# Which four PSUM sums stay in place across the value phases of a product-key retrieval kernel, and which bank the rotation takes first

## Chip, core and metric

The kernel runs on 1 core of one Trainium2 chip. The metric is the device time of one execution in microseconds (us). TensorE is PE in the rows (PEld for its weight loads), VectorE is DVE, ScalarE is ACT, GpSimd is POOL, SyncE is SP. PSUM has eight banks; a bank holds 512 float32 per partition.

## What is computed

One decoder layer with a gated recurrence, a short convolution and, after them, a retrieval from 16384 single-neuron experts. The change lies in the retrieval:

```python
def block(xb):                                  # 128 tokens at a time
    ...                                         # top 16 experts of each of 8 heads: idx, and their softmax gate
    u = expert_u[idx]
    v = expert_v[idx]
    act = gelu(einsum('td,thkd->thk', xb, u))
    return einsum('thk,thkd->td', gate * act, v)
```

1024 tokens, width 1024, all in float32; products are made of halves (a rounded high part and the rest), so each product of two matrices is three matmuls.

## The kernel before

The first 672 tokens are handled densely: for each of 128 blocks of 128 experts the kernel multiplies all 672 tokens with the block's `u` rows, applies Gelu, multiplies with a mostly empty matrix of gates, and multiplies the result W with the block's `v` rows. The other 352 tokens are handled by gathering each token's own rows (`L1084` on POOL, two kinds of row products on DVE in `L1094` and `L1102`); this work runs beside the dense work, in five row buffers.

The dense stage, about 1264 to 2964 us of the profile, alternates two things on PE.

- **U blocks** (`u_steps`, `L1163`): for one block of experts two groups of 24 matmuls, one over 384 tokens and one over 288 (the two parts of `SPL`), each in a bank of the pool `pa`, which has two banks. ACT reads each with Gelu (`L1168`) into the tile `Wl`. Forty of the blocks (`EARLIES`) were done earlier and are loaded from DRAM (`ged`). Then DVE multiplies with the gates (`L1384`), ACT makes the high half `Wh` (`L115`) and DVE the low half `Wl` (`L116`).
- **Value phases** (`v_phase`, `L1403`): for three blocks of experts, 16 groups, one for each token part j and each 128 columns c of the width, of 9 matmuls each (three blocks, three products of halves). The order is j = 0, c = 0 to 7 (384 tokens), then j = 1, c = 0 to 7 (288 tokens). Here they are called groups 0 to 15.

A phase comes between two U blocks, one block behind, so that two (late in the stage three) U blocks lie between phases. Four of the 16 groups are in `FIXED`: each has a bank of its own (`pacc`) and goes on summing through all phases, and DVE has nothing to do for it until the end. The other twelve take a bank in turn from `new_pv`, alternately one of the two `pa` banks and one of the two `pv` banks, and DVE adds each to its sum in SBUF (`L1419`); until that is done, the bank is not free. So a `pa` bank is used by U blocks and phases in turn, and a `pv` bank by phases alone.

Each engine works off its own queue in order. The order in those queues comes from a scheduler in the compiler's tile layer, which places instructions by its own estimate of when they can start. The gathering work is handed out along the dense matmuls (`along`, `advance`).

Of the kernel before, what the change touches and what calls it, by code (L numbers as in the profile page):

```python
# [61 lines left out]
WB = 2  # L62
WJ = 0
PAIRS = [(0, 2), (2, 4)]
FIXED = [(0, 1), (0, 5), (1, 1), (1, 5)]
RB = 0.15
RD = 0.0
DG = 2
# [31 lines left out]
def build(tc, A, out, dbg=None):  # L100
# [41 lines left out]
    with root:  # L142
# [1200 lines left out]
        while u_early(1.0, "G"):  # L1343
# [7 lines left out]
        accs = {(j, c): mp.tile([P, n], F32, name=f"acc{j}{c}") for j, (_, n) in enumerate(SPL) for c in range(KC)  # L1351
                if (j, c) not in FIXED}
        fixed = {f: psM.tile([P, 512], F32, name=f"pacc{f[0]}{f[1]}", bufs=1) for f in FIXED}

        turn = [0]

        def new_pv():

# [182 lines left out]
```

## Time and profile before

| | |
|---|---|
| time, median of 3 runs (lowest to highest) | 2999.6 us (2998.78 to 3002.16) |
| the profiled execution's own time | 2986.61 us |
| its span, first to last instruction | 2984.8 us |
| busy in the span: PE, DVE, ACT, POOL | 95%, 85%, 31%, 29% |
| dense stage, 1264 to 2968 us: PE busy, DVE busy | 1629.70, 1526.58 of 1704.00 us |
| granted TensorE clock in that stage | 0.99 of full speed |

Busy time of PE counts matmuls as pipelined, so it is not work at its peak. A wait shown for an engine is idle time just before an instruction, with the instruction that ended it; waits of PEld and PE for the same thing lie over each other and are not added.

### The profile page before, as it was taken

To read this page: it belongs to the slowest core of one execution; us is meant where nothing else is said; L and a number is where in the kernel's file an instruction comes from. 1 tells how busy PE (TensorE), PEld (TensorE's weight loads), DVE (VectorE), ACT (ScalarE), POOL (GpSimd) and SP (SyncE) were. 2 spreads that over 40 slices of the span, in tenths; PEclk is the share of its full clock that TensorE was granted. 3 is DMA by queue.
4 is the path that set the end of the run, shared out by engine and by line. 5 is a ranking of instruction groups with operands and counts; after the bars stand their busy time and mean duration, and the time that the engine had idled before them with its cause. 6 is when DMAs were issued, how large, how long until landed. Compare 5 with 4: busy or idle time off the path is not lost.

```text
span 2984.8 us, 47174 instructions
## 1 busy us (share of the span) xinstructions
PE 2850.0 (95%) x18190; PEld 2687.0 (90%) x18190; DVE 2547.3 (85%) x5369; ACT 939.3 (31%) x1548; POOL 862.6 (29%) x726
## 2 busy tenths in 40 slices
PE   8999999989999999999999999999899999899998
PEld 6887898878999889999999999999899999899998
DVE  6885549988999987488999989889899988899998
ACT  5643645333222455422222222222222222222222
POOL 0000000000000000045554544445454554555451
PEclk9999999989999999999999999999999999999999
DMA  7424342244223687788889989899899998899995
GB/s 271 146 90 140 127 155 64 78 141 146 70 90 112 212 253 244 246 307 323 324 324 330 340 321 340 325 323 332 304 351 327 329 324 316 311 327 329 324 320 182
DMA packets 288676, 740.01 MB, mean 248 GB/s; under 512 B 27873, under 2 KB 122081, under 8 KB 282050
## 3 DMA queue, kind: packets, MB, share of 16 engines
q0 software_dynamic: 102944, 374.78, 35.3%
q1 hardware_dynamic: 185506, 362.22, 35.3%
q8 instruction: 142, 2.33, 0.3%
q14 instruction: 84, 0.69, 0.1%
HBM read 666.29 MB, written 70.52 MB: 247 GB/s over the span
## 4 chain that ended last, share of the span: by engine, by line
issue 27%; DVE 25%; DMA 20%; PE 20%; POOL 5%; ACT 2%; SPq 0%; DVEq 0%; POOLq 0%; ACTq 0%
PE pp L469 5%; DVE gacc L1094 5%; DMA wl<-in_uT 3%; DVE wl L116 3%; DVE acc L1419 3%; DMA Wl<-ged 2%; PE pq L875 2%; PE pp L875 2%; DVE vl L116 2%; DVE Wl L1384 1%; DMA more<-in_u,idx 1%; PE pa L1163 1%; PE ps L579 1%; PE pp L380 1%; POOL more L1084 1%
## 5 line engine op out<-in xcount | busy, mean ns | idle before, releaser
L1163 PE MATMUL pa<-h2h,wh 128*128 128x384 f32 (+1 forms) x1840 | 590.3, 321 | 14.2 <-DVE acc L1419 12.0
L1163 PE MATMUL pa<-h2l,wh 128*128 128x384 f32 (+1 forms) x1840 | 588.0, 320 | 0.0
L1163 PE MATMUL pa<-h2h,wl 128*128 128x384 f32 (+1 forms) x1840 | 584.0, 317 | 2.7 <-DVE wl L116 2.7
L1163 PEld LDWEIGHTS pa<-h2h,wh 128*128 128x128 f32 x1840 | 347.9, 189 | 19.4 <-DVE acc L1419 13.3
L1163 PEld LDWEIGHTS pa<-h2h,wl 128*128 128x128 f32 x1840 | 349.0, 190 | 2.9 <-DVE wl L116 2.9
L1163 PEld LDWEIGHTS pa<-h2l,wh 128*128 128x128 f32 x1840 | 349.7, 190 | 0.0
L115 ACT ACTIVATE Wh<-Wl 128x672 fp32r<-128x672 f32 x128 | 98.0, 766 | 754.4 <-PE pv L1403 487.9
L115 ACT ACTIVATE wh<-wl 128x1024 fp32r<-128x1024 f32 x187 | 197.7, 1057 | 385.6 <-DMA wl<-in_uT 187.1
L1403 PE MATMUL pa<-Wh,vh 128*128 128x384 f32 (+1 forms) x768 | 251.5, 327 | 53.6 <-ACT Wl L1168 41.7
L116 DVE TENSOR_TENSOR wl<-wl,wh 128x1024 fp32r<-128x1024 f32 x187 | 228.0, 1219 | 75.3 <-ACT wh L115 74.6
L1403 PE MATMUL pv<-Wh,vh 128*128 128x384 f32 (+1 forms) x768 | 245.4, 320 | 5.2 <-DVE acc L1419 4.9
L1403 PE MATMUL pa<-Wl,vh 128*128 128x384 f32 (+1 forms) x768 | 245.8, 320 | 0.7 <-DVE Wl L116 0.7
L1403 PE MATMUL pa<-Wh,vl 128*128 128x384 f32 (+1 forms) x768 | 245.6, 320 | 0.0
L1403 PE MATMUL pv<-Wh,vl 128*128 128x384 f32 (+1 forms) x768 | 243.7, 317 | 0.0
L1403 PE MATMUL pv<-Wl,vh 128*128 128x384 f32 (+1 forms) x768 | 243.3, 317 | 0.0
L1403 PEld LDWEIGHTS pa<-Wh,vh 128*128 128x128 f32 x768 | 145.7, 190 | 67.7 <-ACT Wl L1168 52.1
L115 ACT ACTIVATE vh<-vl 128x1024 fp32r<-128x1024 f32 x128 | 134.4, 1050 | 125.5 <-DMA vl<-in_v 75.5
L1403 PE MATMUL pacc<-Wh,vh 128*128 128x384 f32 (+1 forms) x512 | 163.6, 320 | 1.5 <-ACT vh L115 1.5
L1403 PE MATMUL pacc<-Wh,vl 128*128 128x384 f32 (+1 forms) x512 | 163.7, 320 | 0.6 <-DVE vl L116 0.6
L1403 PE MATMUL pacc<-Wl,vh 128*128 128x384 f32 (+1 forms) x512 | 163.0, 318 | 0.0
L116 DVE TENSOR_TENSOR vl<-vl,vh 128x1024 fp32r<-128x1024 f32 x128 | 155.7, 1217 | 3.2 <-ACT vh L115 3.2
L469 PE MATMUL pp<-h1h,wh 128*128 128x512 f32 x384 | 157.3, 410 | 0.0
(1944 smaller groups left out, 7405.8 us busy)
## 6 DMA issues: line engine op xcount, KB each, us to landing
wl<-in_uT SPq DMA_DIRECT2D x128, 512.0 KB, 5.9
vl<-in_v SPq DMA_DIRECT2D x128, 512.0 KB, 7.9
gd<-stg SPq DMA_DIRECT2D x21, 2048.0 KB, 9.3
gsb<-gd SPq DMA_DIRECT2D x32, 1344.0 KB, 9.1
wl<-in_win SPq DMA_DIRECT2D x48, 512.0 KB, 3.5
wa<-in_wada SPq DMA_DIRECT2D x16, 1024.0 KB, 5.0
wl<-in_wq SPq DMA_DIRECT2D x32, 512.0 KB, 3.5
ged<-ge SPq DMA_DIRECT2D x40, 336.0 KB, 3.1
```

Source lines behind the costliest of these rows:

```text
L115: C.activation(hi, src, AF.Copy)
L116: V.tensor_tensor(lo, src, hi.bitcast(F32), op=OP.subtract)
L380: T.matmul(pvs[t], l[:, t * P:(t + 1) * P], r, start=(k == 0 and l is h1[0][k] and r is wi[0]), stop=(k == KC - 1 and l is h1[1][k]))
L469: T.matmul(pp, l[:, k], r[k], start=(i == 0), stop=(i == 3 * KC - 1))
L579: T.matmul(ps_[:, c], X[:, cs_], Y[:, cs_], start=True, stop=True)
L875: T.matmul(pq[:, :m], l[:, k], hs[k, r][:, o:o + m], start=(i == 0), stop=(i == 3 * KC - 1))
L1084: G.indirect_dma_start(out=r, out_offset=None, in_=src, in_offset=IndirectOffsetOnAxis(ap=idx[:n, s0 + j:s0 + j + 1], axis=0))
L1094: V.scalar_tensor_tensor(ac, r, aw[:, j:j + 1], ac, op0=OP.mult, op1=OP.add))
L1163: T.matmul(pa[:, :n], l[:, k], h2[k, r][:, o:o + n], start=(i == 0), stop=(i == 3 * KC - 1))
L1384: V.tensor_tensor(gv, gv, gs[b // GB][:, :, b % GB], op=OP.mult)
L1403: T.matmul(pv[:, :n], l[:, c * P:(c + 1) * P], r[:, o:o + n], start=(i == 0 and (not fx or b0 == 0)), stop=(i == 3 * (b1 - b0) - 1 and (no ...
L1419: V.tensor_tensor(a, a, pv[:, :n], op=OP.add)
```

## The change

Two constants. The four fixed groups are (j, c) = (0, 0), (0, 1), (1, 6), (1, 7), so groups 0, 1, 14 and 15 of a phase, and no longer groups 1, 5, 9 and 13. And the turn starts at 1, so that a phase's first rotating group takes a `pv` bank and not a `pa` bank.

```diff
-FIXED = [(0, 1), (0, 5), (1, 1), (1, 5)]
+FIXED = [(0, 0), (0, 1), (1, 6), (1, 7)]
...
-        turn = [0]
+        turn = [1]
```

No instruction is added or removed; the order in the queues changes. Before, the rotating groups of a phase are 0, 2, 3, 4, 6, 7, 8, 10, 11, 12, 14, 15 and take pa, pv, pa, pv and so on; now they are groups 2 to 13 and take pv, pa, pv, pa and so on.

The first place is PE at the start of a phase: the last matmul of the U blocks, and the first of each of the first groups. Before:

```order
L1163 MATMUL pa<-h2h_86,wl 128x288
L1403 MATMUL pa<-Wh,vh 128x384
...
L1403 MATMUL pacc_13127<-Wh,vh 128x384
...
L1403 MATMUL pv<-Wh,vh 128x384
```

Now:

```order
L1163 MATMUL pa<-h2h_86,wl 128x288
L1403 MATMUL pacc_13127<-Wh,vh 128x384
...
L1403 MATMUL pacc_13128<-Wh,vh 128x384
...
L1403 MATMUL pv<-Wh,vh 128x384
...
L1403 MATMUL pa<-Wh,vh 128x384
```

The first `pa` bank of a phase was that of group 0 and is that of group 3.

The second place is DVE between the U blocks and the first add of a phase (the phase that begins at 1943.31 us in the profile of before). `Wl<-Wl,gsb` is the product with the gates, `Wl<-Wl,Wh` the low half of W, `wl` and `vl` low halves of `u` and `v`, `grow` and `more` are gathered rows. Before:

```order
L1384 TENSOR_TENSOR Wl<-Wl,gsb 128x672
L1102 SCALAR_TENSOR_TENSOR grow__19770,aw<-grow__19770,hx 128x1024
L116 TENSOR_TENSOR Wl<-Wl,Wh 128x672
L1102 SCALAR_TENSOR_TENSOR grow__19786,aw<-grow__19786,hx 128x1024
L1102 SCALAR_TENSOR_TENSOR grow__19802,aw<-grow__19802,hx 128x1024
L116 TENSOR_TENSOR vl<-vl,vh 128x1024
L116 TENSOR_TENSOR wl<-wl,wh 128x1024
L1384 TENSOR_TENSOR Wl<-Wl,gsb 128x672
L1419 TENSOR_TENSOR acc_13115<-acc_13115,pa 128x384
```

Now:

```order
L1384 TENSOR_TENSOR Wl<-Wl,gsb 128x672
L1102 SCALAR_TENSOR_TENSOR grow__19770,aw<-grow__19770,hx 128x1024
L1102 SCALAR_TENSOR_TENSOR grow__19786,aw<-grow__19786,hx 128x1024
L116 TENSOR_TENSOR Wl<-Wl,Wh 128x672
L1102 SCALAR_TENSOR_TENSOR grow__19802,aw<-grow__19802,hx 128x1024
L116 TENSOR_TENSOR vl<-vl,vh 128x1024
L1102 SCALAR_TENSOR_TENSOR more,aw<-more,hx 128x1024
L1384 TENSOR_TENSOR Wl<-Wl,gsb 128x672
L1102 SCALAR_TENSOR_TENSOR grow__19850,aw<-grow__19850,hx 128x1024
L116 TENSOR_TENSOR Wl<-Wl,Wh 128x672
L116 TENSOR_TENSOR wl<-wl,wh 128x1024
L1419 TENSOR_TENSOR acc_13115<-acc_13115,pv 128x384
```

The first add stands three instructions later, and the first `Wl<-Wl,Wh`, the half that the phase itself needs, stands one row product later.

## Rows read from the trace of the kernel before

**Rows 1.** The stage 1264 to 2968 us: length, then busy us per engine.
```profile
1264.00:2968.00 1704.00, 1629.70 (x10334) 1605.08 (x10335) 1526.58 (x2169) 390.80 (x559) 847.95 (x698) 0.99 0.89 320
```

**Rows 2.** Waits in the dense stage: engine, waiter, releaser: us, times, longest.
```profile
PEld pa L1403 <- ACT Wl L1168: 52.1, 41, 3.2
PE pa L1403 <- ACT Wl L1168: 41.7, 34, 3.0
PEld pa L1403 <- DVE acc L1419: 15.1, 14, 2.6
PEld pa L1163 <- DVE acc L1419: 13.3, 4, 6.4
PEld pv L1403 <- DVE acc L1419: 8.3, 14, 1.7
```

**Rows 3.** PE in order of time, round one phase: start, duration, engine, line, instruction, idle before.
```profile
1932.79 0.34 PE L1163 MATMUL pa<-h2h,wh 128*128 128x384 f32 x1
...
1937.01 0.29 PE L1163 MATMUL pa<-h2h,wh 128*128 128x288 f32 x1
...
1940.05 0.29 PE L1163 MATMUL pa<-h2h,wl 128*128 128x288 f32 x1
1943.31 0.44 PE L1403 MATMUL pa<-Wh,vh 128*128 128x384 f32 x1 [2.96 <-ACT Wl L1168]
...
1944.99 0.34 PE L1403 MATMUL pacc<-Wh,vh 128*128 128x384 f32 x1
...
1946.58 0.34 PE L1403 MATMUL pv<-Wh,vh 128*128 128x384 f32 x1
...
1956.10 0.29 PE L1403 MATMUL pa<-Wh,vh 128*128 128x288 f32 x1
...
1957.30 0.30 PE L1403 MATMUL pacc<-Wh,vh 128*128 128x288 f32 x1
...
2106.77 0.44 PE L1403 MATMUL pa<-Wh,vh 128*128 128x384 f32 x1 [2.23 <-ACT Wl L1168]
```

**Rows 4.** ACT in order of time, before the same phase.
```profile
1941.17 0.76 ACT L115 ACTIVATE Wh<-Wl 128x672 fp32r<-128x672 f32 x1 [4.95 <-DVE Wl L1384]
1941.84 1.04 ACT L115 ACTIVATE vh<-vl 128x1024 fp32r<-128x1024 f32 x1
1942.78 0.47 ACT L1168 ACTIVATE Wl<-pa 128x384 f32<-128x384 f32 x1
```

**Rows 5.** DVE in order of time, the same phase's low half and first add.
```profile
1942.20 0.85 DVE L116 TENSOR_TENSOR Wl<-Wl,Wh 128x672 fp32r<-128x672 f32 x1
...
1948.30 0.54 DVE L1419 TENSOR_TENSOR acc<-acc,pa 128x384 f32<-128x384 f32 x1
```

**Rows 6.** DVE in order of time: first and last of the 492 adds.
```profile
1314.92 0.55 DVE L1419 TENSOR_TENSOR acc<-acc,pa 128x384 f32<-128x384 f32 x1
...
2937.86 0.44 DVE L1419 TENSOR_TENSOR acc<-acc,pv 128x288 f32<-128x288 f32 x1
```

**Rows 7.** DVE's groups in the dense stage: count, busy us and mean ns, idle before.
```profile
L1419 DVE TENSOR_TENSOR acc<-acc,pa 128x384 f32<-128x384 f32 (+1 forms) x246 | 122.0, 496 | 1.1 <-PE pa L1403 1.1
L1419 DVE TENSOR_TENSOR acc<-acc,pv 128x384 f32<-128x384 f32 (+1 forms) x246 | 121.9, 496 | 2.1 <-PE pv L1403 2.1
...
L1384 DVE TENSOR_TENSOR Wl<-Wl,gsb 128x672 f32<-128x672 f32 x127 | 108.3, 853 | 40.7 <-DMA Wl<-ged 22.8 <-ACT Wl L1168 17.8
L116 DVE TENSOR_TENSOR wl<-wl,wh 128x1024 fp32r<-128x1024 f32 x85 | 103.7, 1221 | 14.5 <-ACT wh L115 14.4
...
L1102 DVE SCALAR_TENSOR_TENSOR more<-more,hx 128x1024 f32<-128x1024 f32 x69 | 84.2, 1220 | 12.4 <-DMA more<-in_u,idx 12.3
```

## The prediction, made before the changed kernel was run

> **What bounds the kernel now.** I read the busy time by stage first: in the dense stage PE is busy for 1629.7 of 1704 us and DVE for 1526.6 [rows 1], so PE sets the end and DVE is close behind. Only this stage is touched: outside it every queue holds the same instructions in the same order. Next the waits of that stage. PE waits for two things. At the first matmul of a `pa` group of a phase it waits for Gelu (ACT `L1168`) to have read the bank: 52.1 us in 41 waits, counted at the weight load, or 41.7 us in 34 counted at the matmul. And it waits for DVE's add (`L1419`) to free a bank: 15.1 us and 8.3 us in phases, 13.3 us at the U blocks, 36.7 us in all [rows 2]. I use the counts at the weight load, since it waits first. Of the 34 Gelu waits 24 stand at group 0 and 10 at group 3; I went through the phases in the timeline of PE for that.
>
> Then one phase in the timelines. The last U matmul starts at 1940.05 us, and group 0 starts only at 1943.31, after 2.96 us of idle time [rows 3]. The first U half ended at about 1937.0, yet its Gelu starts at 1942.78: ahead of it in ACT's queue stand `Wh`, which waited 4.95 us for DVE's product with the gates, and `vh` [rows 4]. So the wait for Gelu is a wait for DVE, passed on by ACT. The same timeline gives the length of a group: 1.59 us for 384 tokens (1944.99 to 1946.58), 1.19 us for 288 (1956.10 to 1957.30), and 4.22 us for the first U half (1932.79 to 1937.01); the second takes about 3.2 us [rows 3].
>
> DVE comes late everywhere. The first add of this phase ends at 1948.84 [rows 5], while group 0 ended at about 1945.1: 3.7 us late. I took this lag for 480 of the 492 adds [rows 6], from the end of a group to the end of its add, over 40 phases: the medians lie between 3.5 us and 4.8 us by position. DVE waits almost never for PE: 1.1 us and 2.1 us before the adds, against 40.7 us before the products with the gates and 14.5 us before the low halves of u [rows 7].
>
> **The change part by part.** I call cover the time between the end of a group and the next use of its bank.
>
> *Gelu and the first `pa` group.* Before, the cover from the first U half to group 0 was the second U half, 3.2 us. Now it is that and groups 0, 1 and 2: 3.2 + 3 × 1.59 = 8.0 us. From the second half it was groups 0, 1 and 2, 4.8 us, to group 3; now it is groups 0 to 4, 7.9 us, to group 5. The longest wait was 3.0 us [rows 2], so the latest Gelu freed a first-half bank 3.2 + 3.0 = 6.2 us after its last matmul; the longest wait at group 3 was 2.23 us [rows 3], so 4.8 + 2.2 = 7.0 us. Both lie under the new covers. This removes all 52.1 us. Its bounds are -52.1 and 0, the latter if the lag moves elsewhere (rivals).
>
> *W's low half.* The wait for Gelu hid another one. Group 0's ninth matmul needs the low half `Wl` of the phase's third block. In the phase shown DVE ended it at 1942.20 + 0.85 = 1943.05 [rows 5]. Without the wait group 0 would begin at about 1940.2 and come to that matmul, eight steps of 0.175 us on, at 1941.6: 1.4 us too early, and 2.96 - 1.4 = about 1.5 us is all that the phase gains. By the same account a wait of s at group 0 gives back s - 1.5. Over the 24 waits that is 5.6 us. The order now puts one more row product (1.2 us [rows 7]) ahead of this half; taken in full the excess is over 0.3 us, and about 24 us come back. I take 5.6, since the product stands ahead of it in DVE's queue only in some of the phases, and keep 0 and 24 as bounds.
>
> *Banks in the middle of a phase.* Here the change costs. Before, a fixed group stood between every two or three rotating ones and lengthened the cover: from group 6 to 11 it was 1.59 + 3 × 1.19 = 5.2 us, from 7 to 12 it was 4.8 us. Now twelve rotating groups follow each other on four banks: the cover is three groups, 4.8 us early, and 3 × 1.19 = 3.6 us from groups 7, 8 and 9 to 11, 12 and 13. After the phase the first U half keeps 4.8 us (groups 12 to 15), and the second gets 2 × 1.19 + 4.22 = 6.6 us where it had 1.19 + 4.22 = 5.4 us. I laid the twelve measured lags of each of the 40 phases against the covers, in their order, and took for each phase the largest excess, since one wait shifts what comes after it. With the old covers that gives 29.8 us, near the 36.7 us of rows 2; with the new ones 66.3 us. So this part costs 66.3 - 36.7 = +29.6 us if the lags stay.
>
> Do they stay? For: the first add comes after group 2 and no longer after group 0, 3.2 us later. Against: DVE's queue holds more between the last add of a phase and the first of the next. Counted in the order with the durations of rows 7 it is 21.3 us on average against 16.9, while between the first and the last add it is 14.4 against 19.0, where PE now needs 5 × 1.59 + 6 × 1.19 = 15.1 us. These two nearly cancel: 3.2 us of late start, and 2.4 us at the phase's end, against 4.4 us more work. And every microsecond that PE no longer waits at group 0 is one in which DVE does not catch up. So I leave the lags as they are, and bound them at 1.2 us more (the 52.1 us of waits over some 42 phases) and 1.0 us less (the 5.6 us of late starts and ends less the 4.4, rounded down).
>
> The rule that speaks against this part is in the Trainium skill, page "Perfetto Trace Analysis", section "Matmuls": independent groups should rotate through different PSUM banks, so that the evacuation of one overlaps the matmuls of the next. By it the fixed groups, spread out, are part of the rotation, and taking them from the middle costs overlap; it gives no price, and which way the whole goes is decided by the lags above.
>
> *The end.* The last two fixed sums of the last phase are read by ACT and not by DVE, side by side with DVE's last adds: under 1 us, taken as nothing.
>
> **The sum:** -52.1 + 5.6 + 29.6 = -16.9 us. The profiled execution took 2986.6 us, 13 us under the median of 2999.6; I put the difference on the median: 2999.6 - 16.9 = 2982.7, say 2983 us.
>
> **Rivals.**
>
> *Slower: banks come back too late.* With lags 1.2 us longer the same account gives 108.0 us of bank waits: -52.1 + 5.6 + (108.0 - 36.7) = +24.8 us, 3024 us. It decides from about 0.5 us of extra lag, where the bank waits are 83.3 us and the sum is zero. For it: DVE has nothing left over for PE, as the adds' idle time shows [rows 7]. Against it: PE's own waits stop DVE's lag from growing.
>
> *No change: DVE is the bound.* DVE's idle time is 1704.0 - 1526.6 = 177.4 us [rows 1], and every microsecond saved must come out of it. Some 55 us of that stand before the gate products and the low halves of u [rows 7]; most of the rest are waits for gathered rows, whose row buffers are freed by DVE itself, and these don't depend on PE. If DVE's waits stay, PE's waits only move, and the time stays at 2999.6 us.
>
> *Much faster: lags shorter.* With 1.0 us less the bank waits are 39.5 us: -52.1 + 2.8 + 5.6 = -43.7 us, 2956 us.
>
> **How the numbers follow.** A measurement of this kernel can tell about 0.2%, 6 us, from no change. The forecast, 2968 to 2993 us (lags within 0.4 us of today's), gets 0.42; much faster 0.15; no change, 2994 to 3006 us, 0.21; slower 0.22. So faster 0.57, same 0.21, slower 0.22. The range 2952 to 3012 us takes in the no-change case and part of both outer ones.
>
> **What would show it.** In the profile after, the weight loads' waits for Gelu in phases should be near 0 from 52.1 us; the waits for the adds should be 55 to 80 us from 36.7, most of them at groups 10 to 13 of a phase; waits for `Wl` in group 0 should appear, some 5 us or more; DVE's idle time in the stage should fall by what the stage gets shorter. The forecast is wrong if the adds' waits stay under 45 us or pass 85 us, or if W's halves stop group 0 in nearly every phase.

## The result, and the profile after

The changed kernel took 2956.6 us (median) against 2999.6 us: a ratio of 0.9876, 95% interval 0.9852 to 0.9900, 43 us faster by the medians. Two more jobs gave 0.9864 (0.9843 to 0.9884) and 0.9892 (0.9846 to 0.9938), 44 and 37 us by the medians; by the ratios the gain is 1.1 to 1.4%, 32 to 41 us. The forecast was 2983 us, 17 us faster: the right way and inside the wide range, but about two fifths of the gain, and the time lies where the rival "much faster" (0.15) was put and not in the 2968 to 2993 us that got 0.42.

Two executions were disturbed and are in no ratio: the profiled one of the first result (3402 us, granted clock 0.748), so that the profile shown here is that of the same kernel in the second job, and one of 10149 us in x14_after_nogather. The first lines of the profile:

```profile
span 2967.9 us, 47185 instructions
## 1 busy us (share of the span) xinstructions
PE 2854.8 (96%) x18190; PEld 2682.7 (90%) x18190; DVE 2545.4 (86%) x5369; ACT 941.6 (32%) x1548; POOL 885.5 (30%) x726
```

The span is 16.9 us shorter than that of the profile before, and the dense stage ends earlier by as much. That this is just the sum of the forecast, -16.9 us, is chance: its terms came out otherwise (below), and other profiled executions of the changed kernel took 2958 to 2970 us. This is the stage's row, which answers to [rows 1]:

```profile
1264.00:2951.10 1687.10, 1635.77 (x10342) 1601.30 (x10341) 1525.79 (x2169) 393.26 (x559) 870.83 (x698) 0.99 0.90 324
```

DVE does the same work (1525.8 us against 1526.6), in less time: its idle time fell from 177.4 to 161.3 us. PE's waits in the stage, which answer to [rows 2]:

```profile
PEld pv L1403 <- DVE acc L1419: 36.3, 51, 4.4
PE pv L1403 <- DVE acc L1419: 22.1, 29, 4.2
PEld pa L1403 <- DVE acc L1419: 21.3, 39, 2.4
PE pa L1403 <- DVE acc L1419: 10.9, 28, 2.2
PEld pacc L1403 <- DVE Wl L116: 10.0, 9, 2.0
```

The waits for Gelu in the phases are gone, and so are those of the U blocks (`L1163`) for the adds. Those of the phases for the adds rose from 23.4 us (15.1 + 8.3) to 57.6 us, and W's low half now shows, 10.0 us. One phase of PE in order of time, which answers to [rows 3]:

```profile
1968.15 0.29 PE L1163 MATMUL pa<-h2h,wh 128*128 128x288 f32 x1
...
1971.32 0.34 PE L1403 MATMUL pacc<-Wh,vh 128*128 128x384 f32 x1
...
1973.54 0.44 PE L1403 MATMUL pacc<-Wl,vh 128*128 128x384 f32 x1 [0.49 <-DVE Wl L116]
...
1982.16 0.44 PE L1403 MATMUL pv<-Wh,vh 128*128 128x384 f32 x1 [0.30 <-DVE acc L1419]
...
1986.19 0.40 PE L1403 MATMUL pv<-Wh,vh 128*128 128x288 f32 x1 [0.51 <-DVE acc L1419]
...
1989.46 0.40 PE L1403 MATMUL pv<-Wh,vh 128*128 128x288 f32 x1 [0.20 <-DVE acc L1419]
...
1997.12 0.34 PE L1163 MATMUL pa<-h2h,wh 128*128 128x384 f32 x1
```

Group 0 starts 3.17 us after the second U half did, so without a wait, and stops at its ninth matmul for `Wl`, as foreseen; then come small waits for banks in the middle stretch, three of which are shown, and none before the U block at 1997.12. DVE's groups, which answer to [rows 7]:

```profile
L1419 DVE TENSOR_TENSOR acc<-acc,pv 128x384 f32<-128x384 f32 (+1 forms) x246 | 121.9, 495 | 0.9 <-PE pv L1403 0.6
L1419 DVE TENSOR_TENSOR acc<-acc,pa 128x384 f32<-128x384 f32 (+1 forms) x246 | 121.8, 495 | 2.7 <-PE pa L1403 2.7
L1384 DVE TENSOR_TENSOR Wl<-Wl,gsb 128x672 f32<-128x672 f32 x127 | 108.3, 853 | 42.3 <-ACT Wl L1168 20.1 <-DMA Wl<-ged 19.9 <-ACT wh L115 2.2
```

DVE still hardly waits for PE. What fell is its waits for gathered rows, summed over `L1094` and `L1102`: from 102 us to 87 us.

### The profile page after: what moved, and what is told of

Its sections match the earlier page's. It is cut to its first block, busy times and chain, and to the rows that moved or that the text cites. A ratio compares the mean times of both kernels' runs of the same rounds, so it can differ in the third digit from the quotient of the medians.

```text
span 3400.4 us, 47185 instructions
## 1 busy us (share of the span) xinstructions
PE 3371.7 (99%) x18190; PEld 3051.1 (90%) x18190; DVE 2586.8 (76%) x5369; ACT 949.1 (28%) x1548; POOL 858.9 (25%) x726
## 4 chain that ended last, share of the span: by engine, by line
PE 97%; DVE 1%; DMA 1%; ACT 1%; issue 0%; SPq 0%; DVEq 0%; ACTq 0%
PE pa L1163 34%; PE pv L1403 13%; PE pa L1403 13%; PE pp L469 9%; PE pacc L1403 8%; PE pq L875 4%; PE pg L1330 3%; PE pp L875 2%; PE ps L579 2%; PE pp L380 2%; PE pp L716 1%; PE sc L888 1%; PE po L716 1%; DMA woraw<-in_wout 1%; PE ps L716 1%; PE pp L488 1%
## 5 line engine op out<-in xcount | busy, mean ns | idle before, releaser
L1163 PE MATMUL pa<-h2h,wh 128*128 128x384 f32 (+1 forms) x1840 | 660.9, 359 | 0.1
L1163 PE MATMUL pa<-h2l,wh 128*128 128x384 f32 (+1 forms) x1840 | 658.9, 358 | 0.0
L1163 PE MATMUL pa<-h2h,wl 128*128 128x384 f32 (+1 forms) x1840 | 658.0, 358 | 0.0
L1163 PEld LDWEIGHTS pa<-h2h,wh 128*128 128x128 f32 x1840 | 365.6, 199 | 18.1 <-issue 1.1
L1163 PEld LDWEIGHTS pa<-h2l,wh 128*128 128x128 f32 x1840 | 366.0, 199 | 16.4
L1163 PEld LDWEIGHTS pa<-h2h,wl 128*128 128x128 f32 x1840 | 366.4, 199 | 15.9
L1403 PE MATMUL pv<-Wh,vl 128*128 128x384 f32 (+1 forms) x768 | 275.1, 358 | 0.0
L1403 PE MATMUL pv<-Wl,vh 128*128 128x384 f32 (+1 forms) x768 | 275.0, 358 | 0.0
L1403 PE MATMUL pa<-Wh,vl 128*128 128x384 f32 (+1 forms) x768 | 274.9, 358 | 0.0
L1403 PE MATMUL pv<-Wh,vh 128*128 128x384 f32 (+1 forms) x768 | 274.9, 358 | 0.0
L1403 PE MATMUL pa<-Wl,vh 128*128 128x384 f32 (+1 forms) x768 | 274.4, 357 | 0.0
L1419 DVE TENSOR_TENSOR acc<-acc,pv 128x384 f32<-128x384 f32 (+1 forms) x246 | 123.5, 502 | 112.6 <-PE pv L1403 112.0
L1419 DVE TENSOR_TENSOR acc<-acc,pa 128x384 f32<-128x384 f32 (+1 forms) x246 | 123.5, 502 | 75.0 <-PE pa L1403 73.7
```

The costliest lines, as they stand in the source:

```text
L1163: T.matmul(pa[:, :n], l[:, k], h2[k, r][:, o:o + n], start=(i == 0), stop=(i == 3 * KC - 1))
L1403: T.matmul(pv[:, :n], l[:, c * P:(c + 1) * P], r[:, o:o + n], start=(i == 0 and (not fx or b0 == 0)), stop=(i == 3 * (b1 - b0) - 1 and (no ...
L1419: V.tensor_tensor(a, a, pv[:, :n], op=OP.add)
```

## The experiments

The theory that the runs were made to try is that DVE is late because gathered rows come late, and that PE pays for it wherever a bank's cover is shortest; the change then pays because groups without an add let DVE catch up where it is late (rest). The rivals are that it pays because the banks have more cover where it counts (cover), and that the scheduler's other order does it (order).

**The change again (x1_after).** No edit.

> The change as it is, to have a profile of it at full clock. Cover theory (the gain is the Gelu waits that vanish, and the banks' waits grew less than forecast because DVE's adds came earlier): the weight loads' waits for Gelu in phases near 0 from 52.1 us, the waits for the adds (36.7 us before) between 15 and 45 us, the adds' lag over the groups shorter by about 1 us, about 2956 us. Order theory (the scheduler's other order gave DVE fewer waits for rows and halves, PE's banks have little to do with it): DVE's waits for gathered rows fall by 20 us or more, and the adds' lag is as before.

Measured: ratio 0.9864 (0.9843 to 0.9884), 2954.0 us. In the phases Gelu 0, as the cover theory had it, and adds 57.6 us, above its 15 to 45. The lag of the adds, worked out as in the prediction, median in us by group:

```
before   group  0 4.8   2 4.2   3 4.1   4 3.6   6 4.1   7 4.0   8 4.0  10 3.5  11 3.6  12 3.5  14 3.5  15 4.1
after    group  2 3.8   3 3.9   4 4.1   5 3.9   6 3.7   7 3.9   8 3.7   9 3.6  10 3.2  11 2.3  12 2.3  13 2.2
```

It is about as before up to group 9, and 1.2 to 1.9 us shorter at the last three adds of a phase (groups 12, 14, 15 before, 11, 12, 13 now). So the lags didn't stay, and the order theory's "as before" is wrong too. Its 15 us fewer waits for rows are under the 20 it asked for; over four profiles of the change they are 12 to 25 fewer, so this alone doesn't rule it out.

**The turn alone (x2_turn_only).**

```diff
-        turn = [0]
+        turn = [1]
```

> The fixed groups stay at 1, 5, 9, 13; only the turn starts with a bank of the other pool. First pa group is group 2, cover 3.2 + 2 x 1.59 = 6.4 us: Gelu waits near 0. The cover from group 12 to the next first U half falls to 3.6 us and from 15 to the second to 4.2 us: waits at U blocks grow from 13 to 40 us or more. Cover theory: 10 to 20 us faster than before, so that most of the 43 us need the moved sums too. Lag theory (the gain is the late first add, which gives DVE 3.2 us at the start of a phase): no faster than before.

Measured: 1.0020 (1.0001 to 1.0039), not faster, as the lag theory said. Its waits:

```profile
PEld pa L1163 <- DVE acc L1419: 65.0, 38, 10.1
PEld pv L1403 <- DVE acc L1419: 17.3, 15, 3.8
PEld pa L1403 <- DVE acc L1419: 12.4, 25, 2.4
PEld pa L1403 <- ACT Wl L1168: 5.0, 6, 1.4
```

The Gelu waits vanish (5.0 us from 52.1), and the same time appears as waits of the U blocks for the adds (65.0 from 13.3). The 10 to 20 us that the cover theory asked for didn't come: PE's wait moves. But the same edit takes cover from the U blocks (4.8 and 5.4 us become 3.6 and 4.2), so it doesn't show what more cover for Gelu would be worth with nothing taken elsewhere.

**The front alone (x3_front_only).**

```diff
-FIXED = [(0, 1), (0, 5), (1, 1), (1, 5)]
+FIXED = [(0, 0), (0, 1), (1, 1), (1, 5)]
...
-        turn = [0]
+        turn = [1]
```

> Two fixed sums at groups 0 and 1, the other two stay at 9 and 13, turn starts as in the change. Gelu waits gone as in the change, middle covers as before, but groups 14 and 15 rotate again, so the U halves have covers of 3.6 and 4.2 us. Cover theory: Gelu waits 0, waits of U blocks 30 us or more, 15 to 30 us faster than before. If the start of the phase is all of it: 35 to 45 us faster, as the change.

Measured: 0.9966 (0.9951 to 0.9982), 10 us faster by the ratio (12 by the medians), less than the cover theory's 15 to 30. The U blocks wait, with the same short cover as in x2:

```profile
PEld pa L1163 <- DVE acc L1419: 50.7, 33, 6.4
PEld pv L1403 <- DVE acc L1419: 24.3, 20, 2.6
```

**The back alone (x4_back_only).**

```diff
-FIXED = [(0, 1), (0, 5), (1, 1), (1, 5)]
+FIXED = [(0, 1), (0, 5), (1, 6), (1, 7)]
```

> Fixed sums at groups 1, 5, 14, 15, turn as before, so that a phase begins with a pa bank. Cover theory: the Gelu waits stay near 50 us, the waits of the U blocks for the adds (13.3 us) vanish, middle waits as in the change: within 10 us of before. If the end of the phase (DVE's two groups of rest before the U blocks) is what pays: 20 us or more faster than before, with the Gelu waits halved.

Measured: 0.9935 (0.9915 to 0.9955), 19 us faster by the ratio (24 by the medians), with the Gelu waits nearly halved though their cover is that of before:

```profile
PEld pa L1403 <- DVE acc L1419: 30.4, 33, 4.1
PEld pa L1403 <- ACT Wl L1168: 27.0, 25, 3.8
PEld pv L1403 <- DVE acc L1419: 14.2, 28, 2.9
```

Gelu's read of the first U half ahead of a phase ends 2.5 us after that half, on average, against 3.4 before. This fits the rest theory: two groups without an add ahead of the U blocks let DVE catch up, so that its products with the gates, and Gelu behind them on ACT, come earlier. It doesn't prove it, since the waits for adds in the phases rose from 23.4 to 44.6 us in the same run, and DVE can catch up during those too. In sum PE's waits for Gelu, adds and halves of W fell from 91 to 76 us. The front and the back together give 0.34% + 0.65% = 1.0% of the change's 1.1 to 1.4%.

**The moved sums without the turn (x5_fixed_only).**

```diff
-FIXED = [(0, 1), (0, 5), (1, 1), (1, 5)]
+FIXED = [(0, 0), (0, 1), (1, 6), (1, 7)]
```

> The four sums moved as in the change, but the turn starts as before: group 2 takes a pa bank, group 3 a pv bank. The cover for the first U half's Gelu is 3.2 + 2 x 1.59 = 6.4 us and the first U half after the phase has its bank from group 10 and not 11. Rest theory (what pays is DVE's rest at both ends of a phase, not which bank comes first): within 8 us of the change, about 2955 us. Cover theory: Gelu waits of some 5 us and middle waits as in the change: the same to 10 us slower than the change; slower than that would show that the turn matters by itself.

Measured: 0.9900 (0.9879 to 0.9921), 2964.8 us. Its waits:

```profile
PEld pa L1403 <- DVE acc L1419: 33.9, 48, 4.5
PEld pv L1403 <- DVE acc L1419: 19.2, 41, 2.4
PEld pacc L1403 <- DVE Wl L116: 8.3, 7, 2.0
```

They are the change's with `pa` and `pv` exchanged. The moved sums carry most or all of the gain, 32 us by the medians of 37 to 44; what the turn adds isn't resolved (the change's intervals, 0.9843 to 0.9938 in three jobs, overlap this one).

**Without the work on gathered tokens, before (x6_before_norows) and after (x7_after_norows).** The 352 gathered tokens are left out, with their output.

```diff
-            bg["back"] = background()
+            pass
```

> The kernel before without all work on the 352 gathered tokens (their rows aren't gathered, multiplied or stored; the output for these tokens is left out). DVE loses some 870 us of row products. If DVE's lateness is behind PE's waits for Gelu and for the banks: adds' lag under 1.5 us, both kinds of wait together under 15 us from 88.8 us, 90 to 140 us faster than before, PE's length of the dense stage left over. If the covers themselves are too short for Gelu: the Gelu waits stay above 30 us.

> The change without the work on the gathered tokens, as in the run beside it. If the change pays by giving a late DVE room: no difference from the run beside it (within 5 us), since nobody is late. If it pays by something of its own (order, fewer bank switches): still 20 to 45 us faster than the run beside it.

Measured: 0.9540 (0.9521 to 0.9560) and 0.9536 (0.9517 to 0.9555), 2858.9 and 2857.9 us. The stage's rows, the first from the kernel before, the second from the changed one:

```profile
1264.00:2840.00 1576.00, 1576.00 (x10247) 1575.40 (x10246) 713.25 (x1024) 376.47 (x520) 0.00 (x0) 1.00 0.30 107
```

```profile
1264.00:2840.00 1576.00, 1575.95 (x10258) 1575.26 (x10257) 724.31 (x1031) 381.24 (x522) 0.00 (x0) 1.00 0.30 107
```

PE is idle for at most 0.05 us in this stretch, in either order, as expected. The covers of before are long enough for a DVE that is on time, and then the change is worth nothing (1.0 us).

**Row products without gathers, before (x13_before_nogather) and after (x14_after_nogather).** All row products stay on DVE, but read a fixed tile; the gathers, and results that depend on them, are left out.

```diff
-                    G.indirect_dma_start(out=r, out_offset=None, in_=src,
-                                         in_offset=IndirectOffsetOnAxis(ap=idx[:n, s0 + j:s0 + j + 1], axis=0))
...
-                    r = row(A["v"], j)
...
-                            V.scalar_tensor_tensor(ac, r, aw[:, j:j + 1], ac, op0=OP.mult, op1=OP.add))
+                            V.scalar_tensor_tensor(ac, hx, aw[:, j:j + 1], ac, op0=OP.mult, op1=OP.add))
...
-                                V.scalar_tensor_tensor(r, r, 1.0, hx, op0=OP.mult, op1=OP.mult,
+                                V.scalar_tensor_tensor(r, hx, 1.0, hx, op0=OP.mult, op1=OP.mult,
```

> The kernel before with all row products on DVE, but on a fixed tile: no row is gathered (left out, with what depends on it). DVE has the same load and no wait for rows; 366 MB of transfers are gone. If the waits for rows are what makes DVE late: 60 to 110 us faster than before, PE's waits for Gelu and adds under 40 us from 88.8, profiled and other executions within 5 us of each other. If DVE's load alone makes it late: under 40 us faster, PE's waits above 60 us.

> The change, also without the gathers. If the change pays by letting a DVE with late rows catch up: under 12 us faster than the run beside it. If it pays against DVE's load as such (the adds crowd together with the U blocks' halves): 20 to 45 us faster than the run beside it, as with the gathers.

Measured: 0.9585 (0.9545 to 0.9626) and 0.9600 (0.9550 to 0.9651), 2869.7 and 2873.1 us: 126 and 123 us faster than before, and the change no faster than the run beside it. The stage's rows, before and after:

```profile
1264.00:2840.00 1576.00, 1576.00 (x10220) 1572.26 (x10219) 1509.97 (x2121) 380.59 (x540) 0.00 (x0) 1.00 0.32 112
```

```profile
1264.00:2840.00 1576.00, 1576.00 (x10212) 1572.43 (x10211) 1510.17 (x2117) 383.38 (x538) 0.00 (x0) 1.00 0.32 113
```

DVE carries 1510 us of work in 1576 us, 96%, and PE is never idle in this stretch; the adds' lag has medians from 0.5 to 1.9 us in the first and from 0.6 to 1.0 us in the second. DVE's adds now wait for PE, and nearly nothing else does, as in this row of the first:

```profile
L1416 DVE TENSOR_TENSOR acc<-acc,pv 128x384 f32<-128x384 f32 (+1 forms) x246 | 122.6, 498 | 18.5 <-PE pv L1400 18.1
```

So DVE's load alone doesn't make it late, and the change pays nothing against it. The gathers make it late. DVE isn't slower beside them: an add takes 496 ns with and 498 ns without, a product with the gates 853 and 852 ns. The runs don't part two ways in which the gathers may do it: DVE's waits for the rows themselves, and the transfers (369 MB by the two profiles) that slow other loads (the median load of `wl` lands after 5.9 us with them and 3.5 us without, and the waits for `ged`, 22.8 us [rows 7], are gone here too).

The 126 us are more than the 60 to 110 asked for, and more than the 91 us that PE waited. Of the rest, the first phase begins at 1256.0 us and not at 1265.2, and the granted clock in the stage is 1.00 and not 0.99, which is worth some 16 us by an estimate from 1629.7 us of PE [rows 1].

**One fixed sum at the front (x8_one_front) and one at the end (x16_front_mid_end).** Groups 0, 9, 14, 15, and groups 0, 1, 10, 15, with the turn of the change.

```diff
-FIXED = [(0, 1), (0, 5), (1, 1), (1, 5)]
+FIXED = [(0, 0), (1, 1), (1, 6), (1, 7)]
...
-FIXED = [(0, 1), (0, 5), (1, 1), (1, 5)]
+FIXED = [(0, 0), (0, 1), (1, 2), (1, 7)]
```

> Fixed sums at groups 0, 9, 14, 15: the rest at the end is kept, one of the two at the front moves to the middle, where the change's remaining waits are (groups 10 to 13). First pa group is group 2, cover 6.4 us. Cover theory: middle waits fall from 57.6 us to under 35 us, Gelu waits under 5 us, 5 to 20 us faster than the change, about 2940 us. Rest theory (each fixed sum at an end gives DVE its room): half of the front's 12 us is lost, 5 to 10 us slower than the change.

> Fixed sums at groups 0, 1, 10, 15, turn as in the change: the change's remaining waits stand before groups 6 to 13, and one fixed sum goes from the end into that stretch. Cover theory: middle waits fall by half, waits of the U blocks return (cover of the first half 3.6 us): 5 us faster to 10 us slower than the change. Rest theory (DVE's rest at the end pays most, as the run with the back only showed): 10 to 20 us slower than the change.

Measured: 0.9876 (0.9858 to 0.9893), 2959.9 us, and 0.9936 (0.9915 to 0.9956), 2975.7 us. The main waits of the first, then of the second:

```profile
PEld pv L1403 <- DVE acc L1419: 28.9, 31, 2.6
PEld pacc L1403 <- DVE Wl L116: 20.8, 17, 2.4
PEld pa L1403 <- ACT Wl L1168: 8.1, 8, 1.8
```

```profile
PEld pv L1403 <- DVE acc L1419: 31.6, 24, 2.9
PEld pa L1163 <- DVE acc L1419: 28.3, 13, 6.3
```

With one fixed sum fewer at the front the middle waits fall (34.0 us, with 5.1 us of `pa`) as the cover theory asked, but W's low half and Gelu (12.6 us in all, with 4.5 at the U blocks, where under 5 was asked for) take the difference: as fast as the change, neither 5 to 20 us faster nor 5 to 10 us slower. With one fewer at the end the U blocks wait again and 17 us of the gain go, against the change's 2959.2 us in the same job, which the rest theory had said. So the end of a phase pays more than the front. No version beat the change clearly.

These runs don't part DVE's rest at the end from the cover of the bank that the first U half takes after the phase: worked out as in the prediction, it is 3.6 us in x2, x3 and x16, 4.8 before, in the change and in x8, 6.0 in x4 and x5. Cover alone isn't it, since x16 has less than before and is 20 us faster.

The traces hold one more thing that orders these versions: where DVE's row products, and its waits for rows, fall. "Between adds" is from the first add of a phase to its last, "elsewhere" from there to the next phase, both over 40 phases:

```
                    ratio to before    row products   waits for rows, us
                                       between adds   between adds   elsewhere
x2_turn_only        1.0020             400            88             26
before (three)      1                  400            76 to 84       17 to 25
x3_front_only       0.9966             341            66             32
x16_front_mid_end   0.9936             305            56             39
x4_back_only        0.9935             336            33             57
x5_fixed_only       0.9900             277            22             52
x8_one_front        0.9876             307            23             68
change (four)       0.9864 to 0.9892   277            23 to 27       52 to 61
```

The faster versions have fewer of these waits between the adds, where banks wait behind them; more of them fall among the U blocks, where no add waits behind them. This is an order among versions and not an experiment: the place of the sums and the scheduler's order change together in each of them, so rest and order are not parted either.

**More executions (x9_before_look, x11_before_look, x10_after_look, x12_after_look, x15_after_again).** No edits.

> The kernel before once more, for another profile, since its profiled execution (2986.6 us) lay 12 us under the median of its runs. If executions differ by how late DVE is: an execution near 2998 us shows PE's waits for Gelu and adds at some 100 us against 88.8 us, and DVE's waits for gathered rows above 102 us. If they differ by PE's clock or the part before 1264 us: the waits are the same and the stage starts later or has a lower clock.

> A third profile of the kernel before, with the same two readings as the first look: waits near 100 us if executions differ by DVE's lateness, 88.8 us if not.

> The change once more, since its profiled execution (2969.7 us) lay 15 us over the median of its runs. If executions differ by how late DVE is: an execution near 2955 us shows PE's waits for adds and W's halves at 50 to 60 us against 70 us and shorter lags. If not: the same waits.

> A third profile of the change, as the second look: with three of each the sum of PE's waits can be set against the times of the same executions. A straight line through the six points with a slope near 1 would show that these waits are all that the change moves.

> The change beside the next run on the same chip, for the size of the gain: the profiled executions of the change took 2966 to 2970 us, the others 2948 to 2963 us. If that holds, 2950 to 2958 us again, with the profiled one 10 us above; if it was the first chip's: 2965 us or more.

Each profiled execution's own time, PE's waits at the weight load in the stage (Gelu and adds in phases and U blocks, W's high and low halves in phases), what is left, and DVE's waits for gathered rows, in us:

```
                     time    Gelu  adds   W     left     rows
before               2986.6  52.5  36.7   1.9   2895.5   102
x9_before_look       2995.3  50.3  40.8   1.3   2902.9   105
x11_before_look      2990.1  54.2  38.0   1.2   2896.7   104
x1_after             2969.7   0.8  57.6  12.3   2899.0    87
x10_after_look       2969.6   3.3  54.9  14.6   2896.8    87
x12_after_look       2966.0   2.0  46.2  19.2   2898.6    91
x15_after_again      2958.2   2.7  50.9   9.5   2895.1    79
```

What is left lies between 2895 and 2903 us, alike in both kernels: in the profiled executions the difference between the two is in these waits. The straight line through the first six points, which x12 was run for, has a slope of 1.01, set mostly by the distance between the two kernels. The same waits don't tell executions of one kernel apart: x9 took 8.7 us longer than the first profile with only 1.3 us more of them, where some 100 us in all against 88.8 were expected if lateness set executions apart. The profiled executions differ by 2990.7 - 2965.9 = 24.8 us (means of three and four), the medians of all by 37 to 44 us. The profiled ones of the change stood above its median in the second job (2969.7 against 2954.0), those of before under theirs (2986.6 against 2999.6); in the last job the change's profiled execution (2958.2) was no slower than the others (median 2959.2), between what x15 expected either way. Why the executions without a profile show more of the gain stays open. A small part may lie in the granted clock of the whole run: it averages 0.9809 in 43 executions of before without a profile and 0.9837 in 12 of the change, 0.9813 and 0.9825 in the profiled ones; an estimate from these means makes that some 5 us more of a difference.

## Why the prediction was wrong, point by point

- **Gelu's waits vanish:** right, none is left in the phases of 52.1 us (0.8 to 3.3 us stand at U blocks instead). What they are worth by themselves no run shows: in x2 they went too, and cover was lost elsewhere.
- **W's low half:** right in mechanism, foreseen at its place, the ninth matmul of group 0; 7.2 to 12.9 us where 5.6 stood in the sum and 24 was the bound, and 2.3 to 6.3 us more for the high half, which the sum didn't have.
- **The end** was taken as nothing, and no run contradicts it.
- **Banks in the middle:** the step that failed. The forecast said "So I leave the lags as they are" and put 66.3 us of bank waits into the sum, 29.6 more than before. The lags fell by 1.2 to 1.9 us at the last three adds of a phase, and the adds' waits were 46.2 to 57.6 us, mean 52.4, 13.9 more than the mean of before. The account of covers held: fed with the changed kernel's own lags it gives 45 to 51 us in its four profiles. The effects that I let cancel (less foreign work between the adds, a later first add and rest at the end, against more work before the first add) did not cancel. How much of the shorter lags is DVE's earlier work and how much PE's longer waits, which shorten a lag too, isn't shown. The term also took the measured 36.7 us from a computed 66.3; the same account gives 29.8 for before, so that like with like it would have been +36.5 and further off. The signs that I had set for being wrong (adds' waits under 45 or over 85 us) did not show. The rival "lags shorter" had the right sign, and its 2956 us meets the median partly by luck: it has 39.5 us of bank waits, and a gain of 43.7 us that no profiled execution shows.
- **The median:** with the measured terms in place of mine (means of the table) the sum is -50.1 + 12.4 + 13.9 = -23.8 us instead of -16.9, near the 24.8 us by which the profiled executions differ. The remaining 12 to 19 us of the medians' gain is in no profile. The step that failed there is "I put the difference on the median": one profile stood for all executions, and the kernel's runs spread by 20 us and more.
- **The rival "no change":** its premise fits, DVE's lateness paces the stage, but not its conclusion. It took the waits for rows as independent of PE; they fell from 102 to 105 us to 79 to 91 us, and from 76 to 84 to 23 to 27 us between the adds. How the place of the sums shortens and moves them was not shown.
- **The Trainium skill's rule on rotating banks** (page "Perfetto Trace Analysis", section "Matmuls"), which the prediction set against this part: the waits in phases for the adds did grow, from 23.4 to 57.6 us, so the trace agrees with it; more was gained elsewhere.

## What to carry to other kernels

A wait of the busiest engine names where lateness is paid and not where it comes from: follow the releaser's own queue until an engine waits for data. Here that was DVE waiting for gathered rows; cover given to one bank and taken from another only moved PE's wait there. In these runs, groups that need nothing from the late engine were worth most just ahead of the U blocks, and the versions that kept the waits for rows out of the stretch of adds were the fastest.

## What the runs showed that I had not expected

DVE at 96% of the stage (1510 of 1576 us) held up PE by nothing, while at 90% with gathered rows it held it up by 91 us: here the busy share said little about lateness. And with one order on the queues, executions of the kernel before spread from 2982 to 3009 us.
